# Warming products, an earlier first turn of x, and one modulation moved to VectorE, at the head of a decoder layer

## The chip, the cores and the metric

The kernel runs on one core of a Trainium2 chip. Its engines are TensorE (products and turns), VectorE, ScalarE, GpSimd and SyncE (SP here), the last of which mainly issues DMA transfers. The metric is the device time of one execution in microseconds (us); less is better. Three runs of the kernel before took 1384.74, 1384.91 and 1386.92 us, so the median is 1384.91 us.

## The reference

One layer on x of 4096 tokens by 1024 features, with a conditioning vector c:

```
shift, scale, gate = split(SiLU(c) @ w_ada + b_ada, 3)
h    = LN(x) * (1 + scale) + shift
u_a | z_a | glu_b | z_b = split(h @ w_in + b_in)         # 512, 512, 1024, 512 columns
y_a  = (grouped linear of (causal pools of u_a - u_a)) * ls * SiLU(z_a)
y_b  = pointwise(SiLU(LN(conv31(glu(glu_b))))) * SiLU(z_b)
y    = concat(y_a, y_b) @ w_out + b_out
out  = LN(alpha * x + gate * y) * g + b
```

All of it in float32. The products are made from a high and a low part (fp32r) of both operands: three products stand for one.

## The kernel before

The tokens are cut into eight blocks of 512. Features stand on partitions, in eight k-tiles of 128. A first phase makes the glu columns and two of the z chunks for all blocks and stores the modulated x, a second phase reloads it for the other columns, and a third makes the pointwise and output products, with the convolution on VectorE beside them. Only the head of the first phase and the statistics of the second block concern us.

**Head.** TensorE first turns c and the bias rows, then multiplies the `ones` tile with itself 18 times (L129 to 131, `WARM`); nothing reads that bank. Meanwhile x's first 512 tokens (four tiles of 128 tokens, all 1024 features) arrive, VectorE takes their statistics (L246) and ScalarE normalises each whole tile (L410).

The modulation vectors scale and shift come in five blocks of 1, 1, 2, 2 and 2 k-tiles (`mods`, L433). Each sums eight rows of w_ada, weighted with SiLU(c). The first `MOD_ROWS[b]` of the eight are summed on VectorE into `macc` (L195, L198; for the larger blocks the first row on ScalarE, L200). The rest are one-column products on TensorE (L209), and one more product with ones sums over partitions (L210). `close()` ends with the three short VectorE instructions that leave 1 + scale (`s1`), shift (`shc`) and minus shift (`shn`). The rows still to be summed wait in the list `steps`, and `MOD_SPREAD[k]` says how many of them are issued before and behind step k's own VectorE work.

**Steps k = 0 to 7** (L484 to 504), one for each k-tile of x: `mod_turned` makes the modulated high part (ScalarE, L354), its copy less shift (L356) and the low part (VectorE, L357) from the turned x; `cast_w` and L486 split w_in's row block; TensorE makes three groups of six products (L493, L497, L501) for six column chunks, with the turn of the next k-tile (`turn_x`, L77) after the first group and, where due, the next block's modulation ahead of the third. After steps 5 and 6, `w3_cols` splits the two last column chunks of w_in (transfers L455, ScalarE casts L458, VectorE L459).

**What sets the order.** Every instruction passed through `seq(engine, ...)` is issued after the previous one of its engine, so the steps' order is fixed. All other instructions are placed by the planner of the tile framework, by program order and modelled times; SP's transfers are among them. A turned or product tile waits for its PSUM bank: `tp_bank` has two, `acc_bank` four, `s2_bank` two.

**Second block's statistics.** While steps 4 to 7 run, `row_stats(1)` calls `col_stats` for four x tiles: ScalarE sums (L293), VectorE makes minus the mean (L294), ScalarE sums the squares (L298), VectorE makes the variance (L299), GpSimd takes the power -1/2 (L300). The list `leads` puts the sum and the mean of tiles 0 to 3 behind steps 4, 4, 5 and 6. The eight columns are then turned, copied by ScalarE (L306), stored (L307) and read back as a broadcast (L317), with which VectorE normalises and modulates the second block (L325 to 337). After the steps, `glu` (sigmoid on ScalarE, L521) empties the product banks.

Of the kernel before, what the change touches and what calls it, by code (L numbers as in the profile page):

```python
# [17 lines left out]
P = 128  # L18
S = 4096
D = 1024  # L20
# [9 lines left out]
WINDOWS = (2, 4, 8, 16)  # L30
UH = 8
EPS = 1e-5
MOD_ROWS = (5, 6, 7, 8, 8)
MOD_SPREAD = ((2, 7), (0, 6), (1, 3), (0, 4), (0, 3), (0, 3))
BLOCKS = ((0, 1), (1, 2), (3, 2), (5, 1))
EARLY = 2
WARM = 18
GATE_SB = 2
PERSB = (1, 1, 1, 1, 1, 1, 0, 0)
ALPHA = 2.0 ** 0.25  # L40
# [3 lines left out]
def tile_layer(ctx, tc, x, x_t, w_in_t, c, w_ada, b_ada, w_in, b_in, w_pool, b_pool, ls_pool, w_dw, b_dw,  # L44
# [37 lines left out]
    def tp_bank(name):  # L82
        return psa.tile([P, 512], F32, tag="tpb", bufs=2, name=name)

    def s2_bank(name):
        return psa.tile([P, 512], F32, tag="s2b", bufs=2, name=name)

    def after(inst, other, sync=False):
        tc.add_manual_dep(inst.ins, other.ins.name,
                          mybir.DependencyInfo(mybir.DependencyClass.Sync if sync else mybir.DependencyClass.NoSync, mybir.DependencyReason.DATA),  # L90
                          reason="issue order")
# [3 lines left out]
    def seq(engine, inst):  # L95
        if engine in tails:
            after(inst, tails[engine])
        tails[engine] = inst
        return inst
# [26 lines left out]
        nc.vector.tensor_copy(cols[:, c0 : c0 + r0], vps[:, :r0])  # L126

    load_cols((("b_ada", b_ada, 24), ("b_in", b_in, 20)), nc.scalar.dma_start, "a")
    warm = tp_bank("warm")  # L129
    for _ in range(WARM):  # L130
        seq("pe", nc.tensor.matmul(warm[:, :P], ones, ones, start=True, stop=True))
    wdw = cst.tile([P, CW * MC], F32, name="wdw")
    wsum = cst.tile([P, HQ + 1, MC], F32, name="wsum")
    wd3 = wdw.rearrange("p (j m) -> p j m", m=MC)
# [156 lines left out]
    def col_stats(src, n, nmean, rstd, name, lead=None):  # L291
        sm = st.tile([P, 3], F32, tag=f"sm{name[0]}", bufs=4, name=f"sm{name}")
        i = nc.scalar.activation(src, src, AF.Identity, accum_out=sm[:, 0:1])  # L293
        mean = nc.vector.tensor_scalar(nmean, sm[:, 0:1], -1.0 / n, None, op0=ALU.mult)  # L294
        if lead is not None:
            after(i, lead[0])
            after(mean, lead[1])
        nc.scalar.activation(src, src, AF.Square, bias=nmean, accum_out=sm[:, 1:2])  # L298
        nc.vector.tensor_scalar(sm[:, 2:3], sm[:, 1:2], 1.0 / n, EPS, op0=ALU.mult, op1=ALU.add)  # L299
        nc.gpsimd.tensor_tensor(rstd, sm[:, 2:3], mhalf[:, 0:1], op=ALU.pow)  # L300

    def to_rows(pb, cs, dst, name):
# [6 lines left out]
    def row_stats(sb):  # L309
        cs = st.tile([P, 8], F32, tag="cs", bufs=2, name=f"xcs{sb}")  # L310
        for t in range(TT):
            i = sb * TT + t
            xt = x_early[t] if sb == 1 else load_x(i, t % 2)
            col_stats(xt, D, cs[:, t : t + 1], cs[:, 4 + t : 5 + t], f"x{i}", leads[t] if sb == 1 else None)
        to_rows(tp_bank(f"xcp{sb}"), cs, rD[sb], f"x{sb}")
        bc = ph.tile([P, 2, T], F32, tag="tm", bufs=5, name=f"xbc{sb}")
        nc.sync.dma_start(bc, rD[sb].rearrange("(a t) p -> a (t p)", a=2).partition_broadcast(P))  # L317
        return bc
# [27 lines left out]
    def turn_x(tiles, k):  # L346
        pb = tp_bank(f"xt0_{k}")
        for t in range(TT):
            seq("pe", transpose(pb[:, t * P : (t + 1) * P], tiles[t][:, k * P : (k + 1) * P]))
        return pb  # L350
# [56 lines left out]
    xt_next = [load_x(t) for t in range(TT)]  # L407
    for t in range(TT):
        rs = stats_dve(xt_next[t], D, "x", t)
        nc.scalar.activation(xt_next[t], xt_next[t], AF.Identity, bias=rs[:, 1:2], scale=rs[:, 0:1])  # L410
    def wada_home(tag, q):
        return wp.tile([P, 2, 2, 2 * P], F32, tag=tag, bufs=10, name=f"wa4_{q}")

# [33 lines left out]
    first = (8, 12, 9, 13, 10, 14)  # L447
    pss0 = [acc_bank(f"p1_0_{n0}") for n0 in first[:4]] + [s2_bank(f"p1_0_{n0}") for n0 in first[4:]]
    starts = {k0: b for b, (k0, nk) in enumerate(mods)}
    leads = []  # L450

    def w3_cols(q):
        raw = wraw(f"w3r{q}").rearrange("p (k h c) -> p k h c", k=4, h=2)
# [13 lines left out]
    for b, (k0, nk) in enumerate(mods):  # L467
        fs, close = mod_block(b, k0, nk, wad[b])
        closers.append(close)
        if b == 0:  # L470
            for f in fs:
                f()
        else:
            steps += fs
    closers[0]()
    whi = cast_w(0)
    pb = turn_x(xt_next, 0)

    def sums(k, part):
        if k < len(MOD_SPREAD):  # L480
# [3 lines left out]
    for k in range(KT):  # L484
        lo = both(Wg[k][1])[:, :, : 3 * P]
        seq("dve", nc.vector.tensor_tensor(lo, rows[k], whi.bitcast(F32), op=ALU.subtract))  # L486
        sums(k, 0)
        xT.append(mod_turned(pb, k))
        sums(k, 1)
        if k + 1 < KT:  # L490
            whi = cast_w(k + 1)
        for n0, ps in zip(first, pss0):
            seq("pe", nc.tensor.matmul(ps, W[n0][k][0], xT[k][0], start=k == 0, stop=False))  # L493
        if k + 1 < KT:
            pb = turn_x(xt_next, k + 1)
        for n0, ps in zip(first, pss0):
            seq("pe", nc.tensor.matmul(ps, W[n0][k][0], xT[k][1], start=False, stop=False))  # L497
        if k + 1 in starts:
            closers[starts[k + 1]]()
        for n0, ps in zip(first, pss0):  # L500
            seq("pe", nc.tensor.matmul(ps, W[n0][k][1], xT[k][0], start=False, stop=k == KT - 1))  # L501
        leads += [(tails["act"], tails["dve"])] * (0, 0, 0, 0, 2, 1, 1, 0)[k]
        if k in (5, 6):
            w3_cols(k - 5)
    assert not steps
# [389 lines left out]
```

## Time and profile before

| what | value |
|---|---|
| median of three runs | 1384.91 us |
| profiled execution | 1383.35 us |
| its span, first to last instruction | 1381.4 us |
| TensorE busy | 1361.7 us, 99% |
| VectorE busy | 1188.5 us, 86% |
| ScalarE busy | 434.1 us, 31% |
| mean granted clock of TensorE | 0.993 of 2.4 GHz |

The profile was taken in one execution. Its times count from the first instruction; what lies around the span (1.95 us here) belongs to the time of the run. Busy shares are averages over three phases and say little about the head, which is 5% of the span. Products overlap, so that one's duration is longer than the distance to the next.

### The profile page before, as it was taken

How to read it: one execution, taken by the hardware profiler on the slowest of the kernel's cores; microseconds unless marked ns; L12 is line 12 of the kernel's file. 1: busy time of each engine (PE TensorE's matmuls, PEld its weight loads, DVE VectorE, ACT ScalarE, POOL GpSimd, SP SyncE). 2: the span in 40 equal slices, each digit the busy share in tenths (PEclk: the TensorE clock that was granted, in tenths of full speed). 3: DMA queues.
4: the chain of work that ended last, by engine and by line, in shares of the span. 5: the costliest groups of instructions: out<-in, count | busy, mean ns of one | idle time of the engine just before them, and what ended most of it. 6: DMA issues, size and time to landing. Idle time of an engine off the chain costs nothing.

```text
span 1381.4 us, 17276 instructions
## 1 busy us (share of the span) xinstructions
PE 1361.7 (99%) x6109; PEld 1124.7 (81%) x6109; DVE 1188.5 (86%) x2339; ACT 434.1 (31%) x775; POOL 139.4 (10%) x193
## 2 busy tenths in 40 slices
PE   7999999999999999999999999999999999999997
PEld 6788888888888888888888888888888888888886
DVE  5769999999999889999869998668796999997754
ACT  3745654532322341111321123323224131223310
POOL 1001110100000221011110120000111111102101
PEclk8999999999999999999999999999999999999999
DMA  9797857565375586052461535435334434334511
GB/s 313 238 343 274 290 215 271 201 236 198 126 263 191 190 251 218 35 184 76 154 205 64 168 123 191 168 115 177 143 130 158 146 131 161 124 128 135 185 61 76
DMA packets 116552, 243.83 MB, mean 177 GB/s; under 512 B 15154, under 2 KB 49778, under 8 KB 116466
## 3 DMA queue, kind: packets, MB, share of 16 engines
q1 hardware_dynamic: 107184, 209.15, 43.7%
q0 software_dynamic: 9216, 33.56, 7.3%
q8 instruction: 48, 0.79, 0.2%
q14 instruction: 38, 0.31, 0.1%
q10 hardware_dynamic: 66, 0.02, 0.0%
HBM read 156.65 MB, written 86.04 MB: 176 GB/s over the span
## 4 chain that ended last, share of the span: by engine, by line
PE 82%; DVE 9%; DMA 5%; ACT 1%; issue 1%; SPq 1%; DVEq 0%; ACTq 0%
PE po L802 25%; PE p L370 4%; PE p L371 4%; PE p2z L370 4%; PE p2z L371 4%; PE p2u L372 4%; PE p2u L371 4%; PE p2z L372 4%; PE p2u L370 4%; PE p L372 4%; DVE ca L665 2%; PE pw L780 2%; PE pw L779 2%; PE pw L778 2%; PE p2b L371 2%; PE p2b L372 2%
## 5 line engine op out<-in xcount | busy, mean ns | idle before, releaser
L665 DVE SCALAR_TENSOR_TENSOR cx<-cv,wdw,cx 128x257 f32<-128x257 f32 (+1 forms) x240 | 143.0, 607 | 0.2
L665 DVE SCALAR_TENSOR_TENSOR ca<-cx,wsum,ca 128x256 f32<-128x256 f32 (+1 forms) x240 | 142.3, 607 | 0.0
L665 DVE SCALAR_TENSOR_TENSOR ca<-cv,wdw,ca 128x256 f32<-128x256 f32 (+1 forms) x224 | 133.2, 607 | 0.0
L831 POOL TENSOR_TENSOR ors<-ove,mhalf 128x1 f32<-128x1 f32 x32 | 47.9, 1497 | 421.8 <-DVE ove L827 413.4
L825 ACT ACTIVATE ojk<-r,osm 128x1024 bf16<-128x1024 f32 x31 | 35.7, 1151 | 151.5 <-DVE osm L822 151.5
L365 POOL DMA_DIRECT2D x2r<-xD x64 | 34.5, 539 | 467.9 <-PE p2b L372 287.0
L820 DVE SCALAR_TENSOR_TENSOR r<-po,r 128x512 f32<-128x512 f32 x62 | 40.7, 682 | 30.6 <-PE po L802 30.6
L665 DVE SCALAR_TENSOR_TENSOR lx<-lv,wdw,lx 128x257 f32<-128x257 f32 x120 | 57.3, 477 | 0.0
L665 DVE SCALAR_TENSOR_TENSOR la<-lx,wsum,la 128x256 f32<-128x256 f32 x120 | 57.1, 476 | 0.0
L665 DVE SCALAR_TENSOR_TENSOR la<-lv,wdw,la 128x256 f32<-128x256 f32 x112 | 52.5, 477 | 0.1
L300 POOL TENSOR_TENSOR xcs<-smx,mhalf 128x1 f32<-128x1 f32 x28 | 24.0, 859 | 239.1 <-DVE smx L299 206.4
L293 ACT ACTIVATE x<-x 128x1024 f32<-128x1024 f32 x28 | 29.6, 1058 | 57.4 <-DMA x<-in_x_dram 57.1
L336 ACT ACTIVATE x<-xk,shc 128x512 fp32r<-128x512 f32 x56 | 38.0, 721 | 25.3 <-DVE xk L327 23.1
L595 ACT ACTIVATE sz<-p2z,cols 128x512 f32<-128x512 f32 x32 | 22.0, 687 | 73.3 <-PE p2z L372 69.0
L834 DVE SCALAR_TENSOR_TENSOR r<-r,ors,b_bc 128x1024 f32<-128x1024 f32 (+1 forms) x33 | 41.0, 1244 | 2.7 <-POOL ors L831 2.6
L337 DVE SCALAR_TENSOR_TENSOR x<-xk,shc,x 128x512 fp32r<-128x512 f32 x56 | 40.6, 740 | 2.4 <-ACT x L336 2.4
L794 DVE SCALAR_TENSOR_TENSOR r<-r,gbo 128x1024 f32<-128x1024 f32 x32 | 38.9, 1215 | 3.7 <-DMA r<-in_x_dram 3.7
L759 ACT ACTIVATE t<-t,cols 128x512 f32<-128x512 f32 x32 | 23.1, 724 | 60.1 <-DMA t<-tD 52.1
L219 ACT CAST yb<-z 128x512 fp32r<-128x512 f32 x32 | 19.8, 617 | 68.4 <-DVE z L785 58.4
L802 PE MATMUL po<-wo1h,ya 128*128 128x512 f32 x128 | 41.1, 391 | 0.0
L802 PE MATMUL po<-wo0h,ya 128*128 128x512 f32 x128 | 41.0, 390 | 0.0
L602 ACT ACTIVATE u<-p2u,bu 128x512 f32<-128x512 f32 x32 | 22.0, 687 | 59.0 <-PE p2u L372 58.9
(429 smaller groups left out, 4129.7 us busy)
## 6 DMA issues: line engine op xcount, KB each, us to landing
x2r<-xD POOLq DMA_DIRECT2D x64, 512.0 KB, 7.3
xD<-x SPq DMA_DIRECT2D x56, 512.0 KB
x<-in_x_dram SPq DMA_DIRECT2D x32, 512.0 KB
r<-in_x_dram SPq DMA_DIRECT2D x32, 512.0 KB
out_dram<-r SPq DMA_DIRECT2D x31, 512.0 KB
xk<-in_x_t_dram SPq DMA_DIRECT2D x28, 512.0 KB
wa<-in_w_ada_dram SPq DMA_DIRECT2D x32, 256.0 KB
vD<-v SPq DMA_DIRECT2D x32, 256.0 KB
```

Of the source, the lines that this page charges most:

```text
L336: nc.scalar.activation(h2[:, 0, :], z, AF.Identity, bias=shc[:, k : k + 1])
L337: nc.vector.scalar_tensor_tensor(h2[:, 1, :], z, shc[:, k : k + 1], h2[:, 0, :].bitcast(F32), op0=ALU.add, op1=ALU.subtract)
L370: nc.tensor.matmul(ps, w[0], X[0], start=first, stop=False)
L371: nc.tensor.matmul(ps, w[0], X[1], start=False, stop=False)
L372: nc.tensor.matmul(ps, w[1], X[0], start=False, stop=last)
L665: nc.vector.scalar_tensor_tensor(dst, src, wt, dst, op0=ALU.mult, op1=ALU.add)
L794: xg = nc.vector.scalar_tensor_tensor(r, r, ALPHA, gbo, op0=ALU.mult, op1=ALU.add)
L802: mm = nc.tensor.matmul(po[h], lhs, Wo[k][wi][:, h * 512 : (h + 1) * 512], start=(k == 0 and wi == 0 and lhs is yh), stop=last)
L820: nc.vector.scalar_tensor_tensor(r[:, sl], po[h], 1.0, r[:, sl], op0=ALU.mult, op1=ALU.add, accum_out=sm[:, h : h + 1])
L825: nc.scalar.activation(jk, r, AF.Square, bias=sm[:, 2:3], accum_out=ss)
L831: nc.gpsimd.tensor_tensor(rs, ve, mhalf[:, 0:1], op=ALU.pow)
L834: nc.vector.scalar_tensor_tensor(r[:, sl], r[:, sl], rs, b_bc[:, sl], op0=ALU.mult, op1=ALU.add)
```

## The change

`WARM` becomes a pair. 25 products of ones are issued where 18 were, into a bank of another tag, and three more behind step 0's first cast. x's normalisation is done in two slices, the first 128 columns and the other 896, all eight in a fixed order on ScalarE. The turn of k-tile 0 moves ahead of modulation 0. One more row of modulations 0, 1 and 2 is summed on VectorE, by which modulation 2 has all eight rows there; `MOD_SPREAD` is raised by one for steps 0 and 1. The list `ends` replaces `leads`: sums and means keep their places (behind steps 4, 4, 5 and 6), and the squares and variances of tiles 0 to 3, which had no such edge, are put behind steps 5, 7, 7 and 7.

```diff
-MOD_ROWS = (5, 6, 7, 8, 8)
-MOD_SPREAD = ((2, 7), (0, 6), (1, 3), (0, 4), (0, 3), (0, 3))
+MOD_ROWS = (6, 7, 8, 8, 8)
+MOD_SPREAD = ((2, 8), (0, 7), (1, 3), (0, 4), (0, 3), (0, 3))
-WARM = 18
+X_STATS = ((4, 5), (4, 7), (5, 7), (6, 7))
+WARM = (25, 3)
...
-    warm = tp_bank("warm")
-    for _ in range(WARM):
-        seq("pe", nc.tensor.matmul(warm[:, :P], ones, ones, start=True, stop=True))
+    def keep_warm(i):
+        ps = s2_bank(f"warm{i}")
+        for _ in range(WARM[i]):
+            seq("pe", nc.tensor.matmul(ps[:, :P], ones, ones, start=True, stop=True))
+
+    keep_warm(0)
...
+        sq = nc.scalar.activation(src, src, AF.Square, bias=nmean, accum_out=sm[:, 1:2])
+        var = nc.vector.tensor_scalar(sm[:, 2:3], sm[:, 1:2], 1.0 / n, EPS, op0=ALU.mult, op1=ALU.add)
         if lead is not None:
-            after(i, lead[0])
-            after(mean, lead[1])
+            for inst, (act, dve), eng in ((i, lead[0], 0), (mean, lead[0], 1), (sq, lead[1], 0), (var, lead[1], 1)):
+                after(inst, (act, dve)[eng])
...
-        nc.scalar.activation(xt_next[t], xt_next[t], AF.Identity, bias=rs[:, 1:2], scale=rs[:, 0:1])
+        for sl in (slice(0, P), slice(P, D)):
+            seq("act", nc.scalar.activation(xt_next[t][:, sl], xt_next[t][:, sl], AF.Identity,
+                                            bias=rs[:, 1:2], scale=rs[:, 0:1]))
...
+    pb = turn_x(xt_next, 0)
     closers[0]()
     whi = cast_w(0)
-    pb = turn_x(xt_next, 0)
+    keep_warm(1)
...
-        leads += [(tails["act"], tails["dve"])] * (0, 0, 0, 0, 2, 1, 1, 0)[k]
+        ends.append((tails["act"], tails["dve"]))
```

## Rows read from the trace of the kernel before

**Rows 1.** The page: busy us, share of span, instructions, by engine.

```profile
PE 1361.7 (99%) x6109; PEld 1124.7 (81%) x6109; DVE 1188.5 (86%) x2339; ACT 434.1 (31%) x775; POOL 139.4 (10%) x193
```

**Rows 2.** Waits of PE, whole span: who, for what, us in total, times, longest.

```profile
PE p L493 <- ACT x L354: 2.7, 2, 1.9
PE mod L209 <- DMA wa<-in_w_ada_dram: 1.5, 1, 1.5
PE mod L210 <- DVE macc L195: 0.9, 1, 0.9
...
PE wps L77 <- DVE smx L299: 0.3, 1, 0.3
```

**Rows 3.** Stretches of 5 us: busy us (instructions), then granted clock, DMA share, GB/s.

```profile
15.00:20.00 5.00, 4.13 (x18) 3.63 (x18) 2.07 (x7) 2.98 (x4) 0.00 (x0) 0.50 1.14 324
...
35.00:40.00 5.00, 5.00 (x19) 3.96 (x18) 4.84 (x9) 2.61 (x5) 0.00 (x0) 0.66 0.95 304
...
50.00:55.00 5.00, 5.00 (x24) 3.78 (x23) 4.55 (x8) 3.94 (x9) 0.00 (x0) 1.00 1.10 320
55.00:60.00 5.00, 3.13 (x17) 2.45 (x18) 2.40 (x9) 4.97 (x10) 0.55 (x1) 1.00 0.05 14
60.00:65.00 5.00, 4.72 (x24) 3.51 (x22) 3.79 (x13) 5.00 (x12) 0.77 (x2) 1.00 0.77 215
```

**Rows 4.** Timeline of PE: start us, us, instruction, [idle before <- releaser].

```profile
5.82 6.92 PE L131 MATMUL warm<-ones 128*128 128x128 f32 x36
...
19.21 2.93 PE L493 MATMUL p<-x,wg0h 128*128 128x512 f32 x6 [0.87 <-ACT x L354]
...
27.95 1.55 PE L493 MATMUL p<-x,wg1h 128*128 128x512 f32 x6
...
35.52 2.76 PE L493 MATMUL p<-x,wg2h 128*128 128x512 f32 x6
...
70.37 0.50 PE L370 MATMUL p<-x,wg0h 128*128 128x512 f32 x1
...
92.26 0.39 PE L370 MATMUL p<-x,wg0h 128*128 128x512 f32 x1
```

**Rows 5.** Timeline of ACT (ScalarE).

```profile
12.20 3.56 ACT L410 ACTIVATE x<-x,xrs 128x1024 f32<-128x1024 f32 x3 [0.21 <-DVE xrs L244]
...
52.09 0.84 ACT L463 CAST wg6h<-wr 128x768 fp32r<-128x768 f32 x1 [0.23 <-DMA wr<-in_w_in_dram]
53.67 0.41 ACT L458 CAST wg0h<-w3r 128x256 fp32r<-128x256 f32 x1 [0.73 <-DMA w3r<-in_w_in_dram]
...
55.26 1.05 ACT L293 ACTIVATE x<-x 128x1024 f32<-128x1024 f32 x1
...
56.31 1.14 ACT L298 ACTIVATE x<-x,xcs 128x1024 f32<-128x1024 f32 x1
...
58.58 0.76 ACT L354 ACTIVATE x<-xt,shc,s 128x512 fp32r<-128x512 f32 x1
...
68.89 0.25 ACT L306 COPY rowsx<-xcp 8x128 f32<-8x128 f32 x1
69.63 1.27 ACT L521 ACTIVATE sg<-p,cols 128x512 f32<-128x512 f32 x2 [0.49 <-PE p L501]
```

**Rows 6.** Waits in 40 to 75 us: PE's weight load.

```profile
PEld p L370 <- ACT sg L521: 0.3, 1, 0.3
```

**Rows 7.** Timeline of DVE (VectorE).

```profile
13.84 1.01 DVE L195 SCALAR_TENSOR_TENSOR macc<-wa,sc,macc 128x256 f32<-128x256 f32 x2
...
29.20 3.77 DVE L195 SCALAR_TENSOR_TENSOR macc<-wa,sc,macc 128x512 f32<-128x512 f32 x5
...
95.19 2.73 DVE L337 SCALAR_TENSOR_TENSOR x<-xk,shc,x 128x512 fp32r<-128x512 f32 x4
```

**Rows 8.** Timeline of SP's DMA issues.

```profile
69.82 0.33 SPq L307 DMA_DIRECT2D rD<-rowsx  x1
```

**Rows 9.** Stretch of 1 us, columns as in rows 3.

```profile
40.00:41.00 1.00, 1.00 (x6) 0.83 (x5) 0.41 (x1) 1.00 (x2) 0.00 (x0) 1.00 0.05 16
```

More of the change, by code (lines that the diff above doesn't have):

```diff
@@ L294, in col_stats @@
         mean = nc.vector.tensor_scalar(nmean, sm[:, 0:1], -1.0 / n, None, op0=ALU.mult)
+        sq = nc.scalar.activation(src, src, AF.Square, bias=nmean, accum_out=sm[:, 1:2])
+        var = nc.vector.tensor_scalar(sm[:, 2:3], sm[:, 1:2], 1.0 / n, EPS, op0=ALU.mult, op1=ALU.add)
         if lead is not None:
-            after(i, lead[0])
-            after(mean, lead[1])
-        nc.scalar.activation(src, src, AF.Square, bias=nmean, accum_out=sm[:, 1:2])
-        nc.vector.tensor_scalar(sm[:, 2:3], sm[:, 1:2], 1.0 / n, EPS, op0=ALU.mult, op1=ALU.add)
+            for inst, (act, dve), eng in ((i, lead[0], 0), (mean, lead[0], 1), (sq, lead[1], 0), (var, lead[1], 1)):
+                after(inst, (act, dve)[eng])
         nc.gpsimd.tensor_tensor(rstd, sm[:, 2:3], mhalf[:, 0:1], op=ALU.pow)
@@ L313, in row_stats @@
             xt = x_early[t] if sb == 1 else load_x(i, t % 2)
-            col_stats(xt, D, cs[:, t : t + 1], cs[:, 4 + t : 5 + t], f"x{i}", leads[t] if sb == 1 else None)
+            col_stats(xt, D, cs[:, t : t + 1], cs[:, 4 + t : 5 + t], f"x{i}", [ends[k] for k in X_STATS[t]] if sb == 1 else None)
         to_rows(tp_bank(f"xcp{sb}"), cs, rD[sb], f"x{sb}")
@@ L449, in tile_layer @@
     starts = {k0: b for b, (k0, nk) in enumerate(mods)}
-    leads = []
+    ends = []
     def w3_cols(q):
```

## The prediction, on record before the result

> **What bounds the kernel now.** I read the engines' busy shares first, then what TensorE waited for, then the stretch in which it waited, engine by engine. TensorE is busy 99% of the span [rows 1], and nine kinds of waits, 11.7 us in all, stand for it over the whole kernel (the four that matter here: [rows 2]); all but one of 0.4 us lie before 68 us. From its product at 70.37 us on [rows 4] it runs all but gapless. So the change, which touches only the first 70 us and the statistics of the second block of tokens, can move the end in two ways: by when TensorE starts that unbroken run, or by a new gap in it.
>
> The first 70 us have three different limits, which an average hides.
> - Up to about 40 us: TensorE's clock and the first modulations. The granted clock is 0.50 (1.2 GHz) in 15 to 25 us (two rows alike) and 0.66 on average in 35 to 40 us, otherwise 1.00 (2.4 GHz) [rows 3]. Six products took 2.93 us in the first k-step and 1.55 us in the second [rows 4].
> - About 41 to 55 us: DMA. The queues run at a share of 1.10 in 50 to 55 us [rows 3]; ScalarE waits 0.23 us for w_in's row block 6 at 52.09 and 0.73 us for the late columns w3r at 53.67 [rows 5].
> - 55 to 69 us: ScalarE, busy 4.97 and 5.00 of 5 us [rows 3]. It sets when the modulated x of step 6 appears (58.58 us [rows 5]; TensorE idled 1.9 us for it [rows 2]), and it ends with the sigmoid at 69.63 us [rows 5]; that frees the PSUM bank which the unbroken run starts in [rows 6].
>
> **The change part by part.** The sum is made against the profiled execution: span 1381.4 us, 1383.35 us with what lies around it. The median of the three runs is 1384.91, 1.56 higher; I carry the difference over to the median.
>
> *More ones products.* 18 took 6.92 us, each as two records [rows 4]. Seven more cost at most 7 x 0.384 = 2.7 us and end at 15.4 us or sooner. Before, TensorE had nothing to do after 5.82 + 6.92 = 12.74 us and waited 1.5 us for w_ada [rows 2]. So they cost nothing up to 14.3 us, and up to 1.1 us beyond, which the turned columns (next) need anyway. The three later ones, at 0.25 to 0.43 us each, lie in the wait for ScalarE's first modulated tile (2.7 - 1.9 = 0.8 us idle [rows 2]): 0.75 to 1.3 us, so between free and 0.4 us late.
>
> *x's first columns ahead.* The last three normalisations run from 12.20 for 3.56 us, to 15.76, on ScalarE [rows 5]. Each splits into 128 and 896 columns; the price of the split is not in the trace. Below: nothing, as its elements are the same. Above: the cost of another short activation, 0.25 us for rowsx [rows 5], so 0 to 1 us for four. I take 0.1 us each. The last slice is then ready near 15 us, the four turns take about 1 us, and modulation 0 follows within 1 us more; step 0's products start at about 18 us instead of 19.21 [rows 4]. Nothing of DVE or DMA stands behind these turns. The bank taken over from the warm products makes the next turn wait for step 0's low half, which the products behind it wait for as well: nothing to 0.15 us.
>
> *Modulation rows on VectorE.* Modulations 0 and 1 hand one more row of 256 columns each to VectorE (1.01 us for two, so 0.5 each), modulation 2 one of 512 (3.77 / 5 = 0.75 us) [rows 7]: +1.75 us of VectorE. TensorE loses 2, 2 and 4 one-column products. In step 1 VectorE is what TensorE waits for (0.9 us [rows 2]), so there the row costs up to 0.75 us and its removal from TensorE returns up to 0.8: taken as zero.
>
> Added up, the head would bring step 4 forward by some 3 to 4 us: at full clock, step 0's two groups of six save 2 x (2.93 - 1.55) = 2.8 us, step 2's first group (2.76 us [rows 4]) 1.2 us, less what VectorE adds. That is what the edits earn, and **it does not get through**. The same transfers in the same order feed steps 5 to 7, and from 42 us on their queue is full. ScalarE's casts of w3r stand ahead of step 6's modulated x in its fixed order, and they waited for a transfer already [rows 5]. Arriving there 4 us earlier makes these waits longer by 4 us; the casts still begin at about 53.7 and end near 55.3. The unknown: their transfers leave only once step 4's low half is done, and can now leave earlier. As the queue does not run dry before they land, I take no gain; at most they gain the 2.2 us under the second rival.
>
> *The squares moved.* Square 1 stood ahead of step 6's modulated x, and squares 2 and 3 ahead of step 7's last ScalarE instruction; now all three are issued behind that. Each takes 1.14 us [rows 5]. Step 6's x is thus free to come 58.58 - 1.14 = 57.4 us if the sum of tile 2 and square 0 stay before it, or 55.4 us if nothing does; VectorE's variance also no longer stands ahead of modulation 4's shift. Then steps 6 and 7 on TensorE end up to 1.2 to 3.2 us earlier, plus 0.9 us for three waits of 0.3 us in them (the last of rows 2 is one). But the squares are only moved: from 55.26 to the end of the row copy at 68.89 + 0.25 = 69.14 us ScalarE needs 13.9 us, of which some 0.4 us idle, for a transfer. Without the row copy (0.25 us), if the sigmoid goes ahead of it, it can start at 55.26 + 13.9 - 0.4 - 0.25 = 68.5 us, 1.1 us sooner; with the copy ahead, which needs square 3, its variance, its power on GpSimd and a turn (about 1 us together), at 70.0 us, 0.4 us later. What becomes late next is therefore the sigmoid, not step 6. I take 0.7 us sooner, nearer to the first, since the sigmoid's input is ready before that 1 us is over.
>
> *Second block.* Its statistics go by the row copy, SP's store at 69.82 us [rows 8], the broadcast, and VectorE to its modulated x. The four last lows start at 95.19 and take 2.73 us together [rows 7], so that k-tile 4 is ready at 95.9. TensorE begins this block at 92.26 [rows 4] and reaches k-tile 4 after 24 products, (92.26 - 70.37) / 96 = 0.228 us apart, at 97.7 us: 1.8 us of slack. A run that starts 0.7 us sooner and a copy up to 1 us later fit in it. The cost is nothing; were the copy 2 us later, it would be 0.9 us.
>
> **Sum:** -0.7 us (bounds -1.1 and +0.4): 1382.65 for a profiled execution like the one shown, **1384.2** for the median. Within 0.2% (2.8 us, about what a measurement here tells from no change) that is the same.
>
> **Rivals.**
> 1. *TensorE's clock falls in the longer idle before step 6 (slower).* TensorE arrives 3 to 4 us earlier at step 5 and waits there for the same transfers. Idle of 1.5 us near 13 us was followed by 0.50; idle of 1.9 us before step 6 was not [rows 2, 3]. At half clock the products lose half of the time that it lasts (2.76 against 1.55 us for six [rows 4]). The loss is covered by the 2.1 us (1.2 + 0.9) by which TensorE comes ahead of the sigmoid, so it decides from 4.2 us of low clock. Such a stretch took all of 15 to 25 us once, and (1 - 0.66) / 0.5 x 5 = 3.4 us of 35 to 40 us [rows 3]: 3.4 us would cost nothing, 10 us 5 - 2.1 = +2.9, so 1387.8. The Trainium skill, TensorE: Matmul & The Clock Gate, section Why this matters for your kernels, says that idle gaps between bursts of products bring the clock down. By that rule this rival holds whenever the gap grows; the trace has one case for it and one against. Chance 0.13.
> 2. *The transfers come sooner (faster).* In 39 to 42 us the DMA share is 0.36, 0.05 and 0.42 (the middle one: [rows 9]): 2.2 us unused, while SP issued seven tiny vector loads in turn. SP's order is made by the planner; if the changed modulations let it put x's tiles or row block 5 ahead of them, the casts, the sigmoid and the row copy all move up by as much as 2.2 us. For it: the loads belong far later in the program. Against: no transfer is changed. Time: 0.7 + 2.2 = 2.9 us less, 1382.0; with the better order 1381.6. Chance 0.24.
> 3. *The edits earn their full 4 us,* the sigmoid being put ahead of the squares. Then the row copy still has all of ScalarE's 13.9 us before it, and the second block stalls by 4 - 1.8 us: -1.8, 1383.1. It is within 0.2% too. Chance 0.1.
>
> **How the numbers follow.** The forecast has 0.5, with rival 3 (0.1) also within 0.2%. Rival 2 gives 0.24, of which I count 0.21 beyond -2.8 us; rival 1's 0.13 is counted as slower at its full price, and the last 0.03 is for orders elsewhere in the plan. So faster 0.24, same 0.62, slower 0.14. The forecast's own range is 1383.4 to 1386. To leave out no more than 2 in 10 it is widened to 1381.5 (rival 2's far end) and 1387.2 (rival 1 with 8 to 9 us of low clock).
>
> **What would show it.** Right: the ones products end before 15.4 us and the granted clock in 15 to 25 us is above 0.50; ScalarE waits longer than 0.73 us at w3r and its cast still starts between 53 and 54.5; TensorE idles more than 1.9 us in 45 to 60 us; ScalarE is full from 55 to 68 with three squares after step 7's last activation; the sigmoid starts at 68.5 to 70 and TensorE's run at 69.3 to 70.8. Wrong: the cast of w3r starts before 52 us, or a granted clock under 1.00 after 55 us, or a TensorE gap over 1 us after 75 us.

## The result and the profile after

| what | before | after |
|---|---|---|
| median of four runs each, us | 1385.51 | 1394.18 |
| lowest and highest, us | 1384.74, 1386.92 | 1391.68, 1395.44 |
| profiled execution, us | 1383.35 | 1394.81 |
| its span, us | 1381.4 | 1392.7 |

The changed kernel is slower: 1.0053 times the time before, 95% interval 1.0031 to 1.0075. A second session gave 1396.11 against 1384.46 (1.0065, 1.0043 to 1.0087). Each ratio is worked out from the paired runs of its session and need not be the quotient of the two medians. The forecast was 1384.2, its range 1381.5 to 1387.2: wrong in sign and size. Runs of one kernel lie several us apart (all runs of the kernel before in the sessions below: 1382.7 to 1393.9), so differences under 2 us are not resolved.

Three places in the product stream divide the loss of the profiled execution (starts on TensorE, us, from the tiles' own lists). `p1z` is a product bank of the first phase, `pw` one of the third:

| | before | after | difference |
|---|---|---|---|
| first product into `p1z` | 81.4 | 83.8 | +2.4 |
| last product into `p1z` (near the end of the first phase) | 441.9 | 445.3 | +3.4 |
| first product into `pw` (third phase) | 931.8 | 943.1 | +11.3 |

So 3.4 us come early, 7.9 us between the end of the first phase and the third phase, and nothing behind that, since the spans differ by 11.3 too. (The medians are only 8.7 apart: the profiled execution of before lies 2.2 us below its median.) TensorE's waits of the changed kernel name the places (columns as in [rows 2]):

```profile
PE ccp L78 <- POOL ccs L304: 4.7, 1, 4.7
PE xt L78 <- ACT x L415: 4.0, 4, 1.2
PE xcp L78 <- POOL xcs L304: 2.7, 1, 2.7
PE mod L214 <- DVE macc L199: 2.3, 2, 1.9
PE p L500 <- ACT x L358: 2.1, 1, 2.1
PE p L375 <- DVE x L341: 1.1, 1, 1.1
```

Two of them had no counterpart before: the turn `ccp`, a turn of statistics that waits for GpSimd, and a product that waits for VectorE's modulated x (L341). A third, the turn `xcp`, which waits for GpSimd too, grew ninefold. Before, it stood at 66.89 us, twelve products ahead of the run that begins at 70.37 [rows 4]:

```profile
PE xcp L77 <- POOL xcs L300: 0.3, 1, 0.3
```

Here are stretches of 5 us of the changed kernel (columns as in [rows 3]):

```profile
15.00:20.00 5.00, 4.83 (x21) 4.73 (x22) 2.02 (x7) 3.36 (x5) 0.00 (x0) 0.50 1.14 327
20.00:25.00 5.00, 5.00 (x22) 4.09 (x21) 4.52 (x9) 1.45 (x2) 0.00 (x0) 0.68 1.10 365
...
70.00:75.00 5.00, 3.61 (x11) 2.93 (x12) 3.62 (x10) 4.39 (x8) 0.55 (x1) 0.66 0.66 169
835.00:840.00 5.00, 0.79 (x4) 0.33 (x2) 4.51 (x12) 0.69 (x1) 5.00 (x2) 0.90 0.84 303
840.00:845.00 5.00, 4.49 (x12) 3.56 (x13) 0.00 (x0) 0.49 (x2) 0.46 (x1) 0.50 0.23 76
```

The granted clock (third column from the end) falls to 0.50, 1.2 GHz, at both turns. At the second it fell within the wait: in stretches of 1 us it was 1.00 up to 839 us and 0.50 from there. TensorE's timeline of the changed kernel, answering to [rows 4]:

```profile
7.74 2.27 PE L133 MATMUL warm<-ones 128*128 128x128 f32 x18
...
19.18 2.93 PE L500 MATMUL p<-x,wg0h 128*128 128x512 f32 x6
...
71.39 0.37 PE L78 MATMUL xcp<-ident,xcs 128*8 128x128 f32 x1 [2.71 <-POOL xcs L304]
71.42 0.78 PE L374 MATMUL p<-x,wg0h 128*128 128x512 f32 x1
71.99 0.63 PE L375 MATMUL p<-x,wg0h 128*128 128x512 f32 x1
...
840.51 0.37 PE L78 MATMUL ccp<-ident,ccs 128*8 128x128 f32 x1 [4.72 <-POOL ccs L304]
840.54 0.78 PE L374 MATMUL p2u<-x2r,wu0h 128*128 128x512 f32 x1
```

The reader is to see that the turn `xcp` stands in TensorE's queue directly ahead of the first product of the unbroken run (70.37 in [rows 4]), and that this run begins with products 0.43 us apart from 71.99 to 74.12 us, where the kernel before had 0.23. ScalarE and VectorE around it, answering to [rows 5] and [rows 7]:

```profile
54.63 0.41 ACT L464 CAST wg0h<-w3r 128x256 fp32r<-128x256 f32 x1 [0.69 <-DMA w3r<-in_w_in_dram]
...
67.43 1.13 ACT L299 ACTIVATE x<-x,xcs 128x1024 f32<-128x1024 f32 x1
...
69.90 1.26 ACT L528 ACTIVATE sg<-p,cols 128x512 f32<-128x512 f32 x2
```

```profile
69.75 0.69 DVE L573 TENSOR_TENSOR wpl<-wpl,lsb 128x512 f32<-128x512 f32 x1 [2.04 <-DMA wpl<-in_w_pool_dram]
...
70.56 0.14 DVE L300 TENSOR_SCALAR smx<-smx 128x1 f32<-128x1 f32 x1
```

The last square ends at 68.6 us. Its variance, 0.14 us of work, stands on VectorE behind `wpl`, which waits 2.04 us for a transfer, and so runs at 70.56. Power and turn follow at 70.78 and 71.39, the row copy at 72.33 (68.89 before, [rows 5]), and its store on SP at 73.19 (69.82 before, [rows 8]).

GpSimd's timeline around 830 us, first the changed kernel:

```profile
823.96 2.77 POOL L304 TENSOR_TENSOR ccs<-smc,mhalf 128x1 f32<-128x1 f32 x1
826.69 3.24 POOL L369 DMA_DIRECT2D x2r<-xD  x6
829.90 10.55 POOL L304 TENSOR_TENSOR ccs<-smc,mhalf 128x1 f32<-128x1 f32 x2
```

and the kernel before:

```profile
825.12 0.58 POOL L365 DMA_DIRECT2D x2r<-xD  x1
828.40 0.72 POOL L300 TENSOR_TENSOR ccs<-smc,mhalf 128x1 f32<-128x1 f32 x1 [2.70 <-DVE smc L299]
829.51 0.55 POOL L300 TENSOR_TENSOR ccs<-smc,mhalf 128x1 f32<-128x1 f32 x1 [0.39 <-DVE smc L299]
```

The same two powers take 0.72 and 0.55 us before and 10.55 us together after, of which the first takes 10.04. They give the last columns of the fifth convolution block's statistics, for which `ccp` waits. The first ended at 839.94, 0.43 us behind the end of an unbroken row of two-input operations on VectorE (839.51). The power ahead of the issues (823.96), which stood behind two other issues, was long as well.

### The profile page after: what moved, and what is told of

Its sections match the earlier page's. It is cut to its first block, busy times and chain, and to the rows that moved or that the text cites. A ratio compares the mean times of both kernels' runs of the same rounds, so it can differ in the third digit from the quotient of the medians.

```text
span 1392.7 us, 17289 instructions
## 1 busy us (share of the span) xinstructions
PE 1366.5 (98%) x6113; PEld 1126.4 (81%) x6113; DVE 1190.9 (86%) x2342; ACT 440.2 (32%) x781; POOL 145.5 (10%) x193
## 4 chain that ended last, share of the span: by engine, by line
PE 93%; DMA 3%; DVE 1%; POOL 1%; SPq 1%; issue 0%; ACT 0%; DVEq 0%; POOLq 0%; ACTq 0%
PE po L809 25%; PE p L375 7%; PE p L376 7%; PE p L374 7%; PE p2u L376 4%; PE p2u L374 4%; PE p2u L375 4%; PE p2z L376 4%; PE p2z L374 4%; PE p2z L375 4%; PE pw L787 2%; PE pw L785 2%; PE pw L786 2%; PE p2b L374 2%; PE p2b L376 2%; PE p2b L375 2%
## 5 line engine op out<-in xcount | busy, mean ns | idle before, releaser
L672 DVE SCALAR_TENSOR_TENSOR ca<-cx,wsum,ca 128x256 f32<-128x256 f32 (+1 forms) x240 | 145.5, 608 | 0.0
L672 DVE SCALAR_TENSOR_TENSOR cx<-cv,wdw,cx 128x257 f32<-128x257 f32 (+1 forms) x240 | 144.2, 610 | 0.3
L672 DVE SCALAR_TENSOR_TENSOR ca<-cv,wdw,ca 128x256 f32<-128x256 f32 (+1 forms) x224 | 135.8, 608 | 0.0
L672 DVE SCALAR_TENSOR_TENSOR lx<-lv,wdw,lx 128x257 f32<-128x257 f32 x120 | 57.3, 478 | 0.0
L672 DVE SCALAR_TENSOR_TENSOR la<-lx,wsum,la 128x256 f32<-128x256 f32 x120 | 57.1, 476 | 0.0
L304 POOL TENSOR_TENSOR ccs<-smc,mhalf 128x1 f32<-128x1 f32 x32 | 40.0, 1256 | 133.9 <-DVE smc L300 133.7
L672 DVE SCALAR_TENSOR_TENSOR la<-lv,wdw,la 128x256 f32<-128x256 f32 x112 | 53.4, 477 | 0.2
L304 POOL TENSOR_TENSOR xcs<-smx,mhalf 128x1 f32<-128x1 f32 x28 | 19.4, 693 | 249.5 <-DVE smx L300 201.2
L341 DVE SCALAR_TENSOR_TENSOR x<-xk,shc,x 128x512 fp32r<-128x512 f32 x56 | 40.4, 741 | 0.6 <-ACT x L340 0.6
L809 PE MATMUL po<-wo3h,ya 128*128 128x512 f32 x128 | 40.3, 389 | 0.0
L809 PE MATMUL po<-wo4h,yb 128*128 128x512 f32 x128 | 40.2, 390 | 0.0
```

What stands on the lines that cost most here:

```text
L341: nc.vector.scalar_tensor_tensor(h2[:, 1, :], z, shc[:, k : k + 1], h2[:, 0, :].bitcast(F32), op0=ALU.add, op1=ALU.subtract)
L672: nc.vector.scalar_tensor_tensor(dst, src, wt, dst, op0=ALU.mult, op1=ALU.add)
L809: mm = nc.tensor.matmul(po[h], lhs, Wo[k][wi][:, h * 512 : (h + 1) * 512], start=(k == 0 and wi == 0 and lhs is yh), stop=last)
```

## Experiments

In the expectations, theory 1 is that the moved squares carry the loss, through the plan; theory 2 that the head's edits lose by themselves; A to D are about the powers at 830 us.

**The parts, one at a time.** `b_stats` has the squares and variances moved, and no other edit:

```diff
+X_STATS = ((4, 5), (4, 7), (5, 7), (6, 7))
...
+            for inst, (act, dve), eng in ((i, lead[0], 0), (mean, lead[0], 1), (sq, lead[1], 0), (var, lead[1], 1)):
+                after(inst, (act, dve)[eng])
```

> The kernel before with the new edges on squares and variances alone; nothing else of the change. Theory 1 (the squares' edges carry the loss): about as slow as the changed kernel, 1391 to 1396 us, with TensorE waiting over 2 us at the row turn near 70 us, about 1 us more at the second block near 97 us, and over 3 us at the turn of the convolution's statistics near 840 us. Theory 2 (the head's edits carry it): within 2 us of the kernel before, 1384 to 1387 us.

Measured: 1387.34 us against 1385.99 (1.0010, 0.9986 to 1.0034). The median lies between the ranges that the two theories gave. Its waits on TensorE show two of the three from above, and none at `ccp`:

```profile
PE p L372 <- DVE x L338: 2.7, 1, 2.7
...
PE xcp L78 <- POOL xcs L301: 1.4, 1, 1.4
```

Its run of products begins at 69.48 us, 0.9 sooner than before, and its last `p1z` is at 444.8 us, 2.9 later: the second block's wait for VectorE takes back more than was won. So the moved squares alone bring the wait at the second block and an early loss of some 3 us. The large loss needs more.

`a_nostats` is the other half: the whole change, but only the sum and the mean held by steps, as before.

```diff
-X_STATS = ((4, 5), (4, 7), (5, 7), (6, 7))
+X_STATS = (4, 4, 5, 6)
...
```

> The changed kernel without the new edges on squares and variances: 25 + 3 ones products, the split normalisation with the early turn and the moved modulation rows stay. Theory 1: no loss left, 1381 to 1386 us, no TensorE wait over 1 us after 60 us. Theory 2: 1391 us or more.

Measured: 1389.03 (1.0012, 0.9988 to 1.0036), ten runs from 1383.7 to 1393.6. This too lies between the two ranges, and the interval holds both no loss and 5 us. The last `p1z` is at 441.7 us (441.9 before), the powers take 0.55 to 0.73 us, and `ccp` does not wait. In the profiled execution TensorE waits 3.6 us for VectorE's convolution at 613.7 to 617.3 us, behind which the granted clock was 0.50 in 619 to 622 us. Most of what this execution loses lies there; what brings the wait was not found.

The head's edits singly, on the kernel before: the ones products (`b_warm`: `WARM = (25, 3)` and `keep_warm`), the split normalisation with the early turn (`b_split`), the modulation rows (`b_rows`), and the last two together (`b_head`), which was also the candidate for beating both kernels. The lines shown are the turn's in `b_split` and `b_head`.

```diff
...
+    pb = turn_x(xt_next, 0)
     closers[0]()
     whi = cast_w(0)
-    pb = turn_x(xt_next, 0)
```

> The kernel before with the ones products of the changed one (25 and 3, in the other pair of PSUM banks), nothing else. Theory 1 (all of the loss comes with the moved squares): within 1.5 us of the kernel before. Theory 2 (the ones products, which no longer follow the turn of the bias rows and end at 10 us, leave TensorE idle ahead of the first products, and that time is lost): 1.5 to 4 us slower, the granted clock 0.50 up to 25 us.

> The kernel before with the split normalisation and the turns ahead of modulation 0, nothing else. Theory 1 (the head's edits do not get through the transfers; all of the loss comes with the moved squares): 1384.5 to 1387, within 1 us of the kernel before; step 0's products start at 18 to 19.2 us, the cast of w3r at 53 to 55 us. Theory 2 (the head's edits lose by themselves): slower by 2 us or more.

> The kernel before with one more row of modulations 0, 1 and 2 on VectorE, nothing else. Theory 1: within 1.5 us of the kernel before; VectorE's later partial sums make TensorE wait 1 to 2 us at the closing of modulation 2, which ScalarE's casts after the transfers hide. Theory 2 (that wait comes through to the end): 1.5 to 3 us slower.

> The kernel before with the split normalisation, the early turns and the modulation rows, without the moved squares and the added ones products: the parts that cost nothing alone. If they add up: 1382 to 1385, 0.5 to 2 us less than the kernel before; if the transfers hide them: the same within 1 us.

| | us | kernel before beside it | ratio, 95% | last `p1z` | last `p1z` to first `pw` |
|---|---|---|---|---|---|
| `b_warm` | 1390.11 | 1386.16 | 1.0024 (1.0004 to 1.0044) | 443.9 | 492.8 |
| `b_split` | 1385.09 | 1384.46 | 0.9996 (0.9977 to 1.0014) | 442.7 | 490.1 |
| `b_rows` | 1384.74 | 1386.16 | 0.9996 (0.9975 to 1.0017) | 442.9 | 490.9 |
| `b_head` | 1386.91 | 1385.60 | 1.0004 (0.9988 to 1.0020) | 442.2 | 489.8 |
| before, profiled | | | | 441.9 | 489.9 |

Split, rows and both together change nothing that can be resolved. By their interval the ones products cost 0.6 to 6 us, which is theory 2's size, but not its place: their run of products began at 70.60 us, 0.2 later than before, and the clock was low only to about 22 us. In their profiled execution 2.5 us are a wait for the convolution's VectorE work near 617 us, as in `a_nostats`. `b_gap5` (below), which has none of the head's edits, waits 2.4 us for the same, so the ones products need not be what brings it; whether they cost anything stays open. No version beat the kernel before.

**The turn in TensorE's queue.** `a_turn` is the changed kernel with the turn `xcp` held behind the first products of the run. To allow this, the last glu pair also moves ahead of the turn in program order, and the row copy and the second block's first normalisations get high priority (not shown):

```diff
...
+        turn = transpose(pb[:n, :P], cs)
+        if behind is not None:
+            after(turn, behind)
...
```

> The changed kernel; the turn of the second block's statistics is put behind the first 7 products of the last glu pair instead of ahead of them (the far part of the plan changes with it). Theory 1: the wait of 2.7 us near 69 us and the low clock of 71 to 74 us go, and the run of products starts near 70.6 instead of 71.4 us and is 2 to 3 us ahead at 80 us; the second block then waits 1 to 3 us near 96 us. If the row turn's place is of no account, the run still starts at 71 us or later. The total is not foretold, as it hangs on the far part.

Measured: 1399.82 us (1.0099, 1.0068 to 1.0130). A miss: the planner made another order, with waits of 3.0, 2.7 and 2.1 us for VectorE and ScalarE later. The run began at 70.55 instead of 71.42, after 2.78 us of waiting for the sigmoid, and the granted clock in 70 to 75 us was 0.50. So the turn's place is worth about 0.9 us of start in this order. The idle and the low clock behind it come without it too, since step 7's products end 1.9 us earlier (67.04 against 68.98 for their last six) and the sigmoid does not.

**The wait at 840 us.** `a_gap` is the changed kernel, where the fifth block's power goes to a column of its own and VectorE copies it on:

```diff
+        if name[:2] == "c5":
+            nc.gpsimd.tensor_tensor(sm[:, 0:1], sm[:, 2:3], mhalf[:, 0:1], op=ALU.pow)
+            nc.vector.tensor_copy(rstd, sm[:, 0:1])
...
```

> The changed kernel; in the statistics of the convolution's block 5 the power goes into a spare column, and VectorE copies it on, so that VectorE has to wait for GpSimd there; the turn comes 8 products (1.8 us) later in TensorE's order by this, and all else stays in its order. Theory A (GpSimd's power is held off while VectorE runs without a pause): the two last powers take under 2 us together instead of 10.55, the wait of 4.7 us at the turn near 840 us and the fall of the clock behind it go, 5 to 7.5 us faster than the changed kernel: 1386.5 to 1389. Theory B (the turn only stands too early): 1.8 us of the wait goes, 1391 to 1393 us, and the power still takes 10 us.

Measured: 1388.58 (1.0020, 0.9999 to 1.0040), no wait of `ccp`. In its profiled execution the two powers came 1.63 us behind the last issue, so this one does not show whether the copy or the later place helped. To compare on one chip, the changed kernel and `a_gap` ran again, with the same edit on the kernel before (`b_gap5`):

> The changed kernel again, beside its copy with the one rerouted power and beside the kernel before. Theory A (of the 8.7 us lost, the larger part comes at about 840 us, where TensorE waits 4.7 us for two of GpSimd's powers that do not finish while VectorE runs two-input operations without a gap, and then runs at half clock): 1391.5 to 1395.5 again, the turn ccp waiting 3 to 6 us at 838 to 842 us, a power of over 8 us in its record. Theory B (that wait was an accident of the first runs; the plan with the moved squares costs what the moved squares alone cost): 1386 to 1389, no wait for a power over 1 us.

> The changed kernel, where the fifth convolution block's powers go to a column of their own and VectorE copies them on, so that VectorE has a short operation there and the turn stands 8 products later. Theory A: 4 to 8 us faster than the changed kernel timed beside it (1386.5 to 1389.5), no wait of the turn ccp over 0.5 us. Theory B: the same time as the changed kernel, within 2 us.

> The kernel before with the same rerouted powers of block 5. If the powers at 820 to 840 us also cost the kernel before something in part of its runs (its runs lay between 1383.0 and 1392.8): the highest runs fall below 1388 and the median falls 1 to 3 us. If they don't: its median is within 1 us of the kernel before, with runs spread as widely, since the wait is only there with the other plan.

Measured: `after2` 1396.11 (six runs, 1393.4 to 1396.8), `a_gap2` 1388.12 (twelve, 1386.2 to 1392.8): 8.0 us apart, no overlap. The wait is no accident; `after2` has it again, with a first power of 10.04 us:

```profile
PE ccp L78 <- POOL ccs L304: 5.2, 1, 5.2
```

In `a_gap2` the powers stand right behind the issues again. The second one (from 833.34) was held 3.51 us, until 0.5 us behind the start of VectorE's copy, its first operation since 833 us that does not read two inputs:

```profile
832.73 4.12 POOL L305 TENSOR_TENSOR smc<-smc,mhalf 128x1 f32<-128x1 f32 x2
```

```profile
836.36 0.14 DVE L306 COPY ccs<-smc 128x1 f32<-128x1 f32 x1
```

The early loss is there in `after2` as well (last `p1z` at 446.2, 4.3 later than before), but it lies elsewhere: the run begins at 70.15 us at full clock, behind a wait for `xcp` of 2.64 us, and then waits 2.8 us for the second block's modulated x. Two stretches of `after2`:

```profile
70.00:75.00 5.00, 5.00 (x22) 4.12 (x23) 2.31 (x5) 3.57 (x8) 0.55 (x1) 1.00 0.86 239
...
95.00:100.00 5.00, 3.93 (x11) 3.12 (x12) 5.00 (x10) 1.94 (x3) 0.00 (x0) 0.66 1.11 385
```

VectorE is full there, and the clock falls at the second wait instead. `b_stats`, `a_gap2` and `a_x2sync` are alike (waits of 2.7, 2.9 and 2.9 us; 0.67, 0.58 and 0.50 in 95 to 100 us). Over the profiled executions with the moved squares (`a_turn`, with its other order, aside) the early loss is 1.8 to 6.3 us.

`b_gap5` gave 1387.48 against 1384.46 (1.0011, 0.9994 to 1.0027): in the other plan the edit gains nothing, and the spread of the runs stays.

What holds the power was still open. `powers` measures it alone, without the layer: four powers beside loads of VectorE.

```diff
+        seq("dve", nc.vector.tensor_scalar(v, w, 2.0, None, op0=ALU.mult))
+        for k in range(4):
+            seq("pool", nc.gpsimd.tensor_tensor(r[:, k : k + 1], v, mhalf[:, 0:1], op=ALU.pow))
+        for f in ops:
+            f()
```

> Only the disputed cost: no layer is computed (zeros are stored); four of GpSimd's 128x1 powers, released together, beside five loads of VectorE in turn: nothing; 30 two-input operations of 128x256; 30 one-input operations of 128x256; 28 two-input operations with a 128x1 one-input operation after every 7; the 30 two-input ones again. Theory A (a power does not get its operands while VectorE runs two-input operations back to back): about 0.55 us a power beside nothing, 2.2 for the four; beside the 30 two-input ones they end only when these end, 11 to 13 us after their start, both times; beside the others 2 to 5 us, in the mixed case one or more powers at every short operation. Theory B (the 10.55 us of the changed kernel have another cause, such as the DMA issues ahead on GpSimd's queue): 2 to 4 us for the four in every stretch.

Measured: theory A falls. GpSimd's timeline, the case beside 30 two-input operations:

```profile
5.60 3.10 POOL L87 TENSOR_TENSOR rtwo<-v,mhalf 128x1 f32<-128x1 f32 x4 [0.34 <-DVE v L85]
```

0.78 us each, against 0.53 beside nothing (2.11 for four). What the layer had and this had not were, among others, DMA issues directly ahead of the powers (826.69 above). `powers_dma` adds six, and lets VectorE run 19 us:

```diff
+        for k in range(dmas):
+            t = p.tile([P, DH], F32, name=f"t{name}{k}")
+            seq("pool", nc.gpsimd.dma_start(t, xt[k][:, :DH]))
```

> The disputed cost by itself once more (no layer is computed, zeros are stored): one power, six DMA issues and two more powers on GpSimd, beside five loads of VectorE in turn: nothing; 48 two-input operations of 128x256 (19 us); 70 one-input ones; 49 two-input ones with a short one-input operation after every 7; 48 two-input ones without the DMA issues; and the second case again. Theory C (a power that stands right behind DMA issues is held while VectorE runs two-input operations without a gap): with nothing beside, the last two powers take about 1.1 us; beside the two-input ones they end only with these, 8 us or longer in their record, both times; beside the mixed ones 1 to 5 us, ending at a short operation; without the DMA issues 1.6 us. Theory D (DMA issues do not matter; the cause is something else of the layer, such as other transfers or ScalarE): 1 to 3 us in every stretch.

GpSimd's timeline, beside two-input operations (`rtwo`), one-input (`rone`), a short operation after every 7 (`rmix`), and two-input ones without issues (`rplain`):

```profile
9.12 3.23 POOL L91 DMA_DIRECT2D ttwo<-in_x_dram  x6
12.36 15.94 POOL L93 TENSOR_TENSOR rtwo<-v,mhalf 128x1 f32<-128x1 f32 x2
...
32.43 1.20 POOL L93 TENSOR_TENSOR rone<-v,mhalf 128x1 f32<-128x1 f32 x2
...
51.12 1.61 POOL L93 TENSOR_TENSOR rmix<-v,mhalf 128x1 f32<-128x1 f32 x2
...
67.85 1.61 POOL L93 TENSOR_TENSOR rplain<-v,mhalf 128x1 f32<-128x1 f32 x2
```

VectorE's timeline beside the first of these:

```profile
8.28 19.08 DVE L75 SCALAR_TENSOR_TENSOR acc<-a,w,acc 128x256 f32<-128x256 f32 x48
```

One stretch of it (us, then busy VectorE and GpSimd, granted clock, DMA share, GB/s):

```profile
18.00:19.00 1.00, 1.00 (x4) 1.00 (x1) 1.00 0.00 0
```

VectorE's stream ends at 27.36, the first power at 27.8 (15.42 us of the 15.94), the second 0.54 later. The repeat took 15.93. The transfers themselves are over by 18 us (DMA share 0.00) while the power waits on to 27.8, so it does not wait for them. Theory C holds: neither the issues nor the two-input stream alone holds a power; together they do, until VectorE stops. The mixed case took as long as the one without issues (1.61 us for two), so it was not held. `powers_dma2` asks how many issues it takes and what frees the power:

> The same stretch (no layer is computed) in six forms beside 48 two-input VectorE operations each (19 us): one DMA issue ahead of the two last powers; three; six with one short one-input operation 1.6 us into the stretch; six with it 3.6 us in, near the end of the issues; six with it 8 us in, while the power is held; six with two fills of 128x1 in place of the two powers. If the hold comes with any issue: the first power takes 14 to 18 us with one and with three as well. If a short operation frees what is held at that moment: with it 8 us in, the power ends there, after about 4 us; 1.6 us in it changes nothing (15 us); 3.6 us in, 0.8 us or 15 us, as the last issue is ahead of it or behind. If the hold is the power's alone, the fills take under 1 us; if it is any operation's, the first fill takes 15 us.

```profile
24.61 1.55 POOL L96 TENSOR_TENSOR rthreeissues<-v,mhalf 128x1 f32<-128x1 f32 x2
...
45.33 16.00 POOL L96 TENSOR_TENSOR rearly<-v,mhalf 128x1 f32<-128x1 f32 x2
...
65.58 1.61 POOL L96 TENSOR_TENSOR rlate<-v,mhalf 128x1 f32<-128x1 f32 x2
...
84.78 5.17 POOL L96 TENSOR_TENSOR rduring<-v,mhalf 128x1 f32<-128x1 f32 x2
...
103.94 0.15 POOL L94 MEMSET rfill<- 128x1 f32 x2
```

One issue (1.66 us) or three (1.55) do not hold the power, so the hold does not come with any issue. Six do, and a short operation early in them (42.82) changes nothing. One just before their end (65.06, issues to 65.6) prevents the hold. One at 88.61, while the power waits, frees it: the first power ends at 89.1. A fill of 128x1, which reads nothing, is not held. The layer does not agree in two points. The last short operation lay at 829.60, 0.3 us before the issues' end, and did not prevent the hold. And powers right behind only two or three issues were long as well, though some were not: 2.77 us behind two (823.96 above, ending 0.5 us behind the start of a short operation of VectorE), 2.37 behind two in `after2`, 2.05 behind three in the kernel before, but 1.18 and 0.57 behind two in `b_stats` and `a_gap`. The layer's transfers are twice as large (512 KB each, not 256). So six is no measure of what it takes; the number and size of the transfers were not tested further.

The Trainium skill, SBUF — State Buffer, section SBUF: two separate sides, says that VectorE with two SBUF inputs and a GpSimd operation that reads SBUF exclude each other, and that whichever starts first holds the ports for its whole instruction. That the power is held and the fill is not agrees; a wait over 38 VectorE instructions of 0.40 us does not follow from it, nor that DMA issues ahead of the power matter.

The test in the layer is `a_x2sync`, the changed kernel with the last two blocks' reloads of x issued by SP. The edit also gives two tiles of the last block's third-phase convolution other buffers; that phase keeps its length.

```diff
-            nc.gpsimd.dma_start(h2, xD[k][sb].bitcast(F32R))
+            if sb >= 6:
+                nc.sync.dma_start(h2.bitcast(F32), xD[k][sb].bitcast(F32))
+            else:
+                nc.gpsimd.dma_start(h2, xD[k][sb].bitcast(F32R))
...
-            if sb == 6:
+            if sb >= 6:
                 pair = lt.tile(shape, F32, tag="la", bufs=2, name=f"la{sb}_{m}")
...
-        if sb == 6:
+        if sb >= 6:
             v = s2.tile([P, 2 * (HQ + TH + 1)], F32, tag="cv", bufs=2, name=f"lv{sb}_{m}",
...
```

> The changed kernel with the reloads of x for the last two blocks of tokens issued by SP in place of GpSimd, so that no DMA issue stands ahead of the fifth convolution block's powers. VectorE's order around them is nearly the same, and the turn ccp stands 46 instead of 53 products behind the last turn. Theory C: no wait of ccp over 1 us, the powers 0.5 to 1.6 us each, 1386 to 1390. Theory D, or VectorE's operations alone: a wait of 3 us or more, 1391 to 1396.

Measured: 1388.53 against 1385.60 (1.0030, 1.0013 to 1.0048); three of its twelve runs lay at 1394 to 1397. Last `p1z` to first `pw` is 490.9 us (489.9 before, 497.8 in the changed kernel), with no wait of `ccp`. GpSimd around 830 us:

```profile
832.24 1.58 POOL L304 TENSOR_TENSOR ccs<-smc,mhalf 128x1 f32<-128x1 f32 x2 [5.64 <-DVE smc L300]
```

The same powers, beside the same gapless stream of VectorE, take 1.58 us, with no issue ahead of them. The rest, 2.9 us between the medians, lies early: the last `p1z` of its profiled execution is at 447.3 us, 5.4 later than before, with 2.9 us of waiting at the second block, 0.9 for a sigmoid, and the low clock in 95 to 100 us.

## Why the prediction was wrong

- **The ones products:** they ended at 10.0 us, before 15.4 as said. But the bank of another tag let the planner put them ahead of the bias rows' turn, so TensorE stood nearly idle from 10 to 15 us. The clock was 0.50 in 15 to 20 us and 0.68 in 20 to 25: half right.
- **x's first columns:** step 0's products began at 19.18, not at 18. The four turns waited 4.0 us in all for the slices, and modulation 0 then ran at the low clock.
- **Modulation rows:** nothing, as said (`b_rows`). TensorE's waits for `macc` became 2.3 us instead of 0.9 [rows 2], ahead of the full transfer queue that holds up the later steps.
- **The head and the full transfer queue:** the head gained 1.1 us at step 4 (45.92 against 47.06), not 3 to 4, and it did not get through: the cast of w3r began at 54.63, with 53.67 before [rows 5]. So the gain was hidden by the transfers, as said, and its size made no difference. ScalarE's wait at w3r was 0.69 us, not longer than the 0.73 that the sign asked for; the longer wait came one row block earlier (1.67 us at 53.10, with 0.23 before [rows 5]). The transfers did not come sooner: rival 2 is out.
- **The squares moved:** here the forecast failed first. It gave the chain from the last square to the row copy 1 us and weighed it only for ScalarE. The turn's chain was 72.33 - 68.6 = 3.7 us, not 1, because the variance stood on VectorE behind a wait for `wpl`; and TensorE has the turn ahead of the run. The sigmoid came at 69.90, inside 68.5 to 70.0, but the run began at 71.42, outside 69.3 to 70.8.
- **TensorE's clock:** the low clock came, but not where rival 1 put it. The wait before step 6 (2.1 us) was followed by 1.00; at the 2.71 us before the run the clock fell to 0.50 and stayed there until about 74.4 us, and after the 2.64 us at the same place in `after2` it was 1.00. Where rival 1 put it, it came in other runs: `b_head`, `b_rows`, `b_warm` and `a_nostats` waited 2.81, 2.88, 2.96 and 2.48 us before step 6 and had 0.50 in 60 to 61 us. Their runs of products still began at 70.27, 70.29, 70.60 and 70.17 us (70.37 before), so it cost next to nothing, as the prediction reckoned for a short stretch of low clock. In the changed kernel, six products at 0.45 us (2.70 us in all) instead of 0.23 lose 1.3 us. With the 1.05 us of later start that makes the +2.4 us by which the first `p1z` is late (83.8 against 81.4).
- **Second block:** the 1.8 us of slack was read rightly, but from an order that the change did not keep. Before, VectorE normalises the second block from 81.25 us and makes its first low part at 85.64:

```profile
85.64 1.40 DVE L337 SCALAR_TENSOR_TENSOR x<-xk,shc,x 128x512 fp32r<-128x512 f32 x2
```

  In the changed kernel the planner put the load `cv` of the convolution ahead of the broadcast on SP, which then waited for the store of v, and from 85.63 us on it put steps of the convolution (L672) between VectorE's normalisations:

```profile
77.90 0.61 SPq L661 DMA_DIRECT2D cv<-vD  x1
78.61 0.54 SPq L321 DMA_DIRECT2D xbc<-rD  x1
```

```profile
86.78 0.48 DVE L672 SCALAR_TENSOR_TENSOR cx<-cv,wdw,cx 128x257 f32<-128x257 f32 x1
...
95.87 0.74 DVE L341 SCALAR_TENSOR_TENSOR x<-xk,shc,x 128x512 fp32r<-128x512 f32 x1
```

```profile
96.67 0.50 PE L375 MATMUL p<-x,wg0h 128*128 128x512 f32 x1 [1.11 <-DVE x L341]
```

  The first low part came 10.2 us later, of which the row copy accounts for 3.4, and TensorE waited at the block's first low part, not at k-tile 4. Here the wait was 1.1 us, with the run itself later; where the run began sooner it was 2.7 to 2.9 us, and the low clock at it came on top, which the text had no term for. `b_stats` and `after2` have the same order. So "cost nothing" was wrong. The 2.4 us at the run's start and these 1.1 us make 3.5, and 3.4 were measured by the last `p1z`.
- **Orders elsewhere in the plan:** the step that failed by size, 7.9 of the 11.3 us. It had a chance of 0.03 and no price. Only with the moved squares did the planner also order the second phase otherwise: `a_nostats`, `b_warm`, `b_split`, `b_rows` and `b_head` have the kernel before's places of the turns `ccp` in TensorE's stream, `b_stats` has the changed kernel's. In that order, with the head's times too (in `b_stats` alone the powers came 0.92 us behind the issues and were not held), six issues, no pause of VectorE and two powers fall together: 4.72 us of waiting, then twelve products in 5.26 us instead of 2.74. That makes 7.2 us worked out from rows; 7.9 were measured from the last `p1z` to `pw`, and 8.0 between the medians of `after2` and `a_gap2`. Which of the head's edits brings these times together was not tested. The second block's order above belongs to the same step: the forecast took the planner's order everywhere as it was.

Two of the three signs named as wrong did show: a granted clock under 1.00 after 55 us, and gaps over 1 us after 75 us. The third, a cast of w3r before 52 us, did not.

## What to carry to other kernels

Where a planner makes the order, an edge added in the head can move work of 800 us later: compare the two orders for each engine over the whole kernel before pricing an edit at the place where it stands. A small reduction that another engine finishes stalls the whole queue in which its turn stands, so follow each such chain through every queue, the waits of its neighbours included. Keep small GpSimd operations that read SBUF from standing behind GpSimd's own DMA issues while VectorE runs two-input operations: issue those transfers from SP (`a_x2sync`), or give VectorE a short one-input operation there (`a_gap2`).

## What the hardware showed that I had not expected

A 128x1 power took 0.54 us beside nothing, 0.82 beside two-input VectorE operations, and 15.42 behind six DMA issues beside them. By itself, behind one issue or three, it was not held; in the layer, behind two or three, it took 0.57 to 2.77 us. One VectorE operation of 0.14 us freed it. And TensorE's granted clock fell to 1.2 GHz after waits of 2.71 and 4.72 us, but not after 2.64 us in the second run of the same kernel, nor after 2.07 us before step 6. In other runs it fell after 2.48 us and not after 2.65 (`a_nostats`, `b_split`), so the length of the wait alone does not settle it. It was back at 2.4 GHz about 3.0 us after the first of these waits ended, and 5.3 us after the second.
